# Squared deviation from the row mean, 1024 x 4096 in fp32: two tiles of four rows per partition instead of three loads and four stores

## The chip, the core and the metric

The kernel runs on one core of one Trainium2 chip. A core has several engines with instruction queues of their own: VectorE (DVE in the profile) and ScalarE (ACT) compute here, SyncE (SP) issues the transfers, and 16 DMA engines move data between the chip's memory (HBM) and the core's on-chip memory of 128 partitions. TensorE (PE) and GpSimd (POOL) have no part in the work. The metric is device time in microseconds (us) for one launch, the median of the runs.

## The reference

```python
batch, dim = 1024, 4096
x = np.random.randn(batch, dim).astype(np.float32)

def reference(x, axis):            # axis = -1
    mean = np.mean(x, axis=axis, keepdims=True)
    return ((x - mean) ** 2).astype(np.float32)
```

Each row of 4096 numbers has its mean taken off, and the differences are squared. Input and output are 16.78 MB each.

## The kernel before

Each of the 128 partitions holds 8 consecutive rows of `x`, 16 KiB a row, so that a partition's part of `x` is one run of 128 KiB in HBM. Three loads, all issued at the start by SP (line 44), bring two, four and two rows per partition, in runs of 32, 64 and 32 KiB; each goes into a tile of its own, so nothing is loaded twice and no buffer is used again.

Then a loop goes over the 8 rows of a partition in order. For each row:

- VectorE sums the row, with the sign changed (`reduce_sum`, line 52), and multiplies the sum by 1/4096 (`tensor_scalar_mul`, line 55). This gives `neg_mean`, one number per partition.
- ScalarE squares the row in place, with `neg_mean` as its bias (`activation` with Square, line 56).
- After every second row, SP issues a store of the two finished rows (line 64), in runs of 32 KiB per partition. It waits for ScalarE.

So a row passes VectorE, then ScalarE, then SP's queue; VectorE may be rows ahead of ScalarE. The framework puts in the waits and may move instructions on an engine; it keeps the order in which rows are summed. All seven transfers are on SP's one queue, so stores are queued behind all loads.

Of the kernel before, what the change touches and what calls it, by code (L numbers as in the profile page):

```python
# [2 lines left out]

os.environ.setdefault("NEURON_RT_ULTRASERVER_MODE", "4")

# [4 lines left out]

F32 = mybir.dt.float32


@with_exitstack
def kernel(
    ctx: ExitStack,
    tc: tile.TileContext,
    x: bass.AP,
    axis: bass.AP,
    out: bass.AP,  # L20
):


    nc = tc.nc

    B, D = x.shape
    P = nc.NUM_PARTITIONS
    R = B // P
    LOADS = [2, 4, 2]
    S = 2  # L30
    assert B == P * R and sum(LOADS) == R
    inv_d = 1.0 / float(D)

    x_v = x.rearrange("(p r) d -> p (r d)", p=P)
    out_v = out.rearrange("(p r) d -> p (r d)", p=P)

    io = ctx.enter_context(tc.tile_pool(name="io", bufs=1))
    stats = ctx.enter_context(tc.tile_pool(name="stats", bufs=2 * R))

    rows = []  # L40
    r0 = 0
    for i, n in enumerate(LOADS):
        x_tile = io.tile([P, n * D], F32, tag=f"x{i}")
        nc.sync.dma_start(out=x_tile, in_=x_v[:, r0 * D:(r0 + n) * D])  # L44
        rows += [(x_tile, k) for k in range(n)]
        r0 += n

    for r, (x_tile, k) in enumerate(rows):
        row = x_tile[:, k * D:(k + 1) * D]
        neg_sum = stats.tile([P, 1], F32)  # L50
        neg_mean = stats.tile([P, 1], F32)
        nc.vector.reduce_sum(  # L52
            out=neg_sum, in_=row, axis=mybir.AxisListType.X, negate=True
        )
        nc.vector.tensor_scalar_mul(out=neg_mean, in0=neg_sum, scalar1=inv_d)  # L55
        nc.scalar.activation(  # L56
            out=row,
            in_=row,
            func=mybir.ActivationFunctionType.Square,
            bias=neg_mean,  # L60
            scale=1.0,
        )
        if r % S == S - 1:
            nc.sync.dma_start(
                out=out_v[:, (r + 1 - S) * D:(r + 1) * D],
                in_=x_tile[:, (k + 1 - S) * D:(k + 1) * D],
            )


# [1 line left out]
_INS = ['x', 'axis']  # L71
_OUTS = [((1024, 4096), 'float32')]

_NUMBERS = {'axis': -1}


# [26 lines left out]
```

## Time and profile before

| | us |
|---|---|
| median of 3 runs | 84.35 (84.27 to 84.47) |
| the profiled execution, its own time | 84.35 |
| its span, first to last instruction | 82.6 |
| one sum of a row on VectorE, line 52 | 4.41 |
| one scaling of the sum on VectorE, line 55 | 0.146 |
| one square of a row on ScalarE, line 56 | 3.70 |
| the table load of ScalarE | 1.28 |

The span is what the profile's stretches are measured in: time 0 is the first instruction. What the execution's time has beyond it, 1.78 us, lies around the span. "Landing" is when a transfer's last data has been confirmed. A line of a group of instructions reads: line, engine, operation, output <- input, shapes, count, then busy time in all and the mean of one in ns, then how long the engine had sat idle before them and for what. In order of time, the core of the work on the second load looks like this:

```profile
32.14 8.75 DVE L52 TENSOR_REDUCE neg_sum<-x_tile 128x1 f32<-128x4096 f32 x2 [10.41 <-DMA x_tile<-in_x_dram]
40.81 0.14 DVE L55 TENSOR_SCALAR neg_mean<-neg_sum 128x1 f32<-128x1 f32 x1
40.87 4.41 DVE L52 TENSOR_REDUCE neg_sum<-x_tile 128x1 f32<-128x4096 f32 x1
40.98 3.71 ACT L56 ACTIVATE x_tile<-x_tile,neg_mean 128x4096 f32<-128x4096 f32 x1 [12.04 <-DVE neg_mean L55]
```

The first number of a line is its start, the second how long it lasted, both in us. VectorE waited 10.41 us for the second load to land, and ScalarE 12.04 us for the first mean of it.

### The profile page before, as it was taken

To read this page: it belongs to the slowest core of one execution; us is meant where nothing else is said; L and a number is where in the kernel's file an instruction comes from. 1 tells how busy PE (TensorE), PEld (TensorE's weight loads), DVE (VectorE), ACT (ScalarE), POOL (GpSimd) and SP (SyncE) were. 2 spreads that over 40 slices of the span, in tenths; PEclk is the share of its full clock that TensorE was granted. 3 is DMA by queue.
4 is the path that set the end of the run, shared out by engine and by line. 5 is a ranking of instruction groups with operands and counts; after the bars stand their busy time and mean duration, and the time that the engine had idled before them with its cause. 6 is when DMAs were issued, how large, how long until landed. Compare 5 with 4: busy or idle time off the path is not lost.

```text
span 82.6 us, 83 instructions
## 1 busy us (share of the span) xinstructions
DVE 35.4 (43%) x16; ACT 30.7 (37%) x9; POOL 0.2 (0%) x4
## 2 busy tenths in 40 slices
DVE  0000008999500004999999999999300000000000
ACT  0000006000599900000196978979699800000000
POOL 0000000000000000000000000000000000000000
DMA  8698990999999099799879998997998999799790
GB/s 238 270 413 349 508 730 32 508 508 508 508 508 476 32 508 508 317 444 508 254 302 460 492 413 365 508 444 333 492 492 381 397 508 429 333 508 476 333 460 0
DMA packets 1008, 33.55 MB, mean 406 GB/s; under 512 B 112, under 2 KB 112, under 8 KB 112
## 3 DMA queue, kind: packets, MB, share of 16 engines
q1 hardware_dynamic: 1008, 33.55, 96.1%
HBM read 16.78 MB, written 16.78 MB: 406 GB/s over the span
## 4 chain that ended last, share of the span: by engine, by line
DMA 37%; DVE 32%; ACT 4%; ACTq 4%; SPq 0%; issue 0%
DMA x_tile<-in_x_dram 37%; DVE neg_sum L52 32%; ACT x_tile L56 4%; ACTq L98 4%; SPq L44 0%; DVE neg_mean L55 0%
## 5 line engine op out<-in xcount | busy, mean ns | idle before, releaser
L52 DVE TENSOR_REDUCE neg_sum<-x_tile 128x1 f32<-128x4096 f32 x8 | 35.0, 4411 | 23.2 <-DMA x_tile<-in_x_dram 23.2
L56 ACT ACTIVATE x_tile<-x_tile,neg_mean 128x4096 f32<-128x4096 f32 x8 | 29.4, 3704 | 22.3 <-DVE neg_mean L55 22.3
L56 ACT ACT_TABLE_LOAD x1 | 1.3, 1283 | 12.8 <-DMA x_tile<-in_x_dram 12.8
L55 DVE TENSOR_SCALAR neg_mean<-neg_sum 128x1 f32<-128x1 f32 x8 | 1.1, 146 | 0.0
L84 POOL MEMSET const-bfloat16-1.0<- 128x1 bf16 x1 | 0.1, 101 | 0.0
L84 POOL MEMSET const-uint8-127<- 128x1 uint8 x1 | 0.1, 101 | 0.0
L84 POOL MEMSET const-float32-0.0<- 128x1 f32 x1 | 0.1, 98 | 0.2 <-issue 0.2
L84 POOL MEMSET const-float32-1.0<- 128x1 f32 x1 | 0.1, 98 | 0.0
## 6 DMA issues: line engine op xcount, KB each, us to landing
out_dram<-x_tile SPq DMA_DIRECT2D x4, 4096.0 KB, 15.1
x_tile<-in_x_dram SPq DMA_DIRECT2D x2, 4096.0 KB, 26.7
x_tile<-in_x_dram SPq DMA_DIRECT2D x1, 31.0
```

The costliest lines, as they stand in the source:

```text
L52: nc.vector.reduce_sum(out=neg_sum, in_=row, axis=mybir.AxisListType.X, negate=True)
L55: nc.vector.tensor_scalar_mul(out=neg_mean, in0=neg_sum, scalar1=inv_d)
L56: nc.scalar.activation(out=row, in_=row, func=mybir.ActivationFunctionType.Square, bias=neg_mean, scale=1.0,)
L84: nc = _bacc.Bacc("TRN2", target_bir_lowering=False, num_devices=1)
L98: with _tile.TileContext(nc) as tc:
```

## The change

The 1024 rows are now cut into two halves of 512. In each half a partition holds 4 consecutive rows, 64 KiB, so that a tile is one block of 8.39 MB in HBM. There are two loads and two stores, each of a whole tile, in runs of 64 KiB.

The work on a tile is shared out differently, and its order on VectorE and ScalarE is fixed by hand (`keep_in_program_order`):

- ScalarE takes the mean of row 3 by itself: an `activation` with Identity copies the row into a scratch tile that nothing reads and puts the row's sum into `total`; a second small one multiplies it by -1/4096.
- VectorE takes the means of rows 0, 1 and 2, as before.
- ScalarE squares rows 3, 0, 1 and the first half of row 2.
- VectorE does the second half of row 2, 2048 elements, in two steps: it adds the negative mean, and multiplies the result by itself.
- SP stores the tile when both engines are through with it.

```diff
-    R = B // P
-    LOADS = [2, 4, 2]
-    S = 2
+    Q = 4
+    H = D // 2
+    ntiles = B // (P * Q)
...
-    x_v = x.rearrange("(p r) d -> p (r d)", p=P)
-    out_v = out.rearrange("(p r) d -> p (r d)", p=P)
+    x_t = x.rearrange("(n p q) d -> n p (q d)", p=P, q=Q)
+    out_t = out.rearrange("(n p q) d -> n p (q d)", p=P, q=Q)
...
+    for i in range(ntiles):
+        x_tile = io.tile([P, Q * D], F32)
+        nc.sync.dma_start(out=x_tile, in_=x_t[i])
+        tiles.append(x_tile)
+
+    inorder = tc.keep_in_program_order
+
+    def mean_on_act(row):
+        copy = scratch.tile([P, D], F32)
+        total = stats.tile([P, 1], F32)
+        neg_mean = stats.tile([P, 1], F32)
+        nc.scalar.activation(
+            out=copy, in_=row, func=ACT.Identity, scale=1.0, accum_out=total
+        )
+        nc.scalar.mul(out=neg_mean, in_=total, mul=-inv_d)
+        return neg_mean
+
+    def mean_on_dve(row):
         neg_sum = stats.tile([P, 1], F32)
         neg_mean = stats.tile([P, 1], F32)
-        nc.vector.reduce_sum(
+        inorder(nc.vector.reduce_sum(
             out=neg_sum, in_=row, axis=mybir.AxisListType.X, negate=True
-        )
-        nc.vector.tensor_scalar_mul(out=neg_mean, in0=neg_sum, scalar1=inv_d)
...
+        ))
+        inorder(nc.vector.tensor_scalar_mul(out=neg_mean, in0=neg_sum, scalar1=inv_d))
+        return neg_mean
+
+    def square_on_act(part, neg_mean):
+        inorder(nc.scalar.activation(
+            out=part, in_=part, func=ACT.Square, bias=neg_mean, scale=1.0
+        ))
+
+    for i in range(ntiles):
+        row = [tiles[i][:, q * D:(q + 1) * D] for q in range(Q)]
+        m3 = mean_on_act(row[3])
+        m0 = mean_on_dve(row[0])
+        square_on_act(row[3], m3)
+        m1 = mean_on_dve(row[1])
+        square_on_act(row[0], m0)
+        m2 = mean_on_dve(row[2])
+        square_on_act(row[1], m1)
+        square_on_act(row[2][:, :H], m2)
+        back = row[2][:, H:]
+        nc.vector.tensor_scalar_add(out=back, in0=back, scalar1=m2)
+        nc.vector.tensor_mul(out=back, in0=back, in1=back)
+        nc.sync.dma_start(out=out_t[i], in_=tiles[i])
```

In what follows, tile A is the first tile (`tiles[0]`, load A, store A) and tile B the second.

More of the change, by code (lines that the diff above doesn't have):

```diff
@@ L11 @@
 F32 = mybir.dt.float32
+ACT = mybir.ActivationFunctionType
 @with_exitstack
@@ L27 @@
     P = nc.NUM_PARTITIONS
-    R = B // P
-    LOADS = [2, 4, 2]
-    S = 2
-    assert B == P * R and sum(LOADS) == R
+    Q = 4
+    H = D // 2
+    assert B % (P * Q) == 0
+    ntiles = B // (P * Q)
     inv_d = 1.0 / float(D)
-    x_v = x.rearrange("(p r) d -> p (r d)", p=P)
-    out_v = out.rearrange("(p r) d -> p (r d)", p=P)
[L37 to L46, printed above, removed]
@@ L48 @@
-    for r, (x_tile, k) in enumerate(rows):
-        row = x_tile[:, k * D:(k + 1) * D]
+    x_t = x.rearrange("(n p q) d -> n p (q d)", p=P, q=Q)
+    out_t = out.rearrange("(n p q) d -> n p (q d)", p=P, q=Q)
+    io = ctx.enter_context(tc.tile_pool(name="io", bufs=ntiles))
+    scratch = ctx.enter_context(tc.tile_pool(name="scratch", bufs=1))
+    stats = ctx.enter_context(tc.tile_pool(name="stats", bufs=2 * ntiles * Q))
+    tiles = []
+    for i in range(ntiles):
+        x_tile = io.tile([P, Q * D], F32)
+        nc.sync.dma_start(out=x_tile, in_=x_t[i])
+        tiles.append(x_tile)
@@ L53 @@
             out=neg_sum, in_=row, axis=mybir.AxisListType.X, negate=True
-        )
[L55 to L67, printed above, removed]
+        ))
```

## The prediction

> **What bounds the kernel now.** I read the DMA rows first, since the kernel reads 16.78 MB and writes 16.78 MB and does little with them.
>
> ```profile
> span 82.6 us, 83 instructions
> DVE 35.4 (43%) x16; ACT 30.7 (37%) x9; POOL 0.2 (0%) x4
> DMA  8698990999999099799879998997998999799790
> q1 hardware_dynamic: 1008, 33.55, 96.1%
> ```
>
> Both compute engines idle for more than half of the span; the one DMA queue keeps its 16 DMA engines occupied for 96.1% of it. (The lower digits in the row of tenths are no gaps: in the packet records, below, each DMA engine goes from packet to packet.) Next, the stretches between the landings, cut where one transfer's packets give way to the next's:
>
> ```profile
> 12.24:31.57 19.33, 8.93 (x4) 8.59 (x3) 0.00 (x0) 1.00 0.96 417
> 31.57:42.35 10.78, 10.21 (x4) 1.37 (x1) 0.00 (x0) 1.00 1.02 398
> 42.35:52.03 9.68, 9.68 (x5) 8.32 (x3) 0.00 (x0) 1.00 1.00 433
> 52.03:61.71 9.68, 6.59 (x5) 8.32 (x3) 0.00 (x0) 1.00 1.00 433
> 61.71:71.39 9.68, 0.00 (x0) 4.13 (x2) 0.00 (x0) 1.00 1.00 433
> ```
>
> The columns are the stretch, its length, the busy time of VectorE, ScalarE and GpSimd, the clock, the DMA share and GB/s. These are load 2 (8.39 MB), load 3 (4.19 MB), and stores 1 to 3 (4.19 MB each). A store takes 9.68 us whatever the engines do; load 2, twice the bytes, takes 19.33. One transfer is out of line: load 3 takes 10.78, that is 1.10 more than a store of the same size. In the trace's packet records (each DMA engine moves 8 packets of a transfer, one for each of its 8 partitions) a 32 KiB packet follows the last after 1.21 us and a 64 KiB one after 2.414, and on all 16 DMA engines only the last two packets of load 3 are long, 1.72 and 1.76 us in the mean instead of 1.21, from 38.7 us until they end at 42.0 to 42.7. What is queued behind them is the first store. I call this place the seam: loads end and stores begin. On the DMA engine that ends last it costs 10.946 - 9.68 = 1.27 us. From the first packet at 1.75 us to the last at 81.41 there is no other idle time in those records; the first packets have 0.65 us extra (1.86 against 1.21).
>
> ```profile
> 0.73 1.33 SPq L44 DMA_DIRECT2D x_tile<-in_x_dram  x3
> SPq L64 <- ACT x_tile L56: 49.1, 4, 16.9
> SPq L64 <- DMA x_tile<-in_x_dram: 13.5, 2, 10.7
> DMA to landing us min/median/max: 23.8/23.8/23.8
> ```
>
> Loads are issued at 0.73 and the first packet moves at 1.75: 1.02 us from issue to data. SP's queue does wait for ScalarE, but the last row (the first store, issued at 28.97) shows that its data is taken by 23.8 us later, behind both loads: these waits are hidden. The chain of waits on the page ends through VectorE and ScalarE (32% and 4%), because it follows the last store back to its issue; that store was issued at 65.9 and its packets began only at 71.4, so that chain is not what sets the end. The bytes and the seam are.
>
> **The change, part by part.**
>
> *Packets.* Before: 48 packets of 32 KiB and 8 of 64 KiB for each DMA engine, 48 x 1.2096 + 8 x 2.4137 = 77.37 us. After: 32 of 64 KiB, 77.24. Gain 0.13, if a 64 KiB store packet goes as a 64 KiB load packet does; no row here shows one.
> The Trainium skill (DMA: Bandwidth & Descriptors, Anatomy of one DMA — SWDGE path) fits 2.0 us fixed for each DMA, on another path than SP's; by it three transfers fewer would save 6 us, an estimate. The rows show no such cost between queued transfers: 4 x 9.68 us for the stores is bytes alone.
>
> *The larger first load.* Load A lands at 12.77 (0.73 + 12.0) + 8 x (2.414 - 1.210) = 22.4 us, load B's packets end at 41.04 to 41.40 and it lands at 41.75, provided that the seam takes nothing from it. Nothing is lost by the later start, since the queue has load B to do.
>
> *Work on tile A*, which now decides when the first store can start. Rows:
>
> ```profile
> L52 DVE TENSOR_REDUCE neg_sum<-x_tile 128x1 f32<-128x4096 f32 x8 | 35.0, 4411 | 23.2 <-DMA x_tile<-in_x_dram 23.2
> L56 ACT ACTIVATE x_tile<-x_tile,neg_mean 128x4096 f32<-128x4096 f32 x8 | 29.4, 3704 | 22.3 <-DVE neg_mean L55 22.3
> L56 ACT ACT_TABLE_LOAD x1 | 1.3, 1283 | 12.8 <-DMA x_tile<-in_x_dram 12.8
> L55 DVE TENSOR_SCALAR neg_mean<-neg_sum 128x1 f32<-128x1 f32 x8 | 1.1, 146 | 0.0
> ```
>
> VectorE: three sums with their scaling, one every 4.39 us (45.26 to 49.64), from 22.44 to 35.6. Then an add and a multiply over 128x2048, of which there is no row. VectorE's 4411 ns for 4096 and 146 for 1 element make 1.04 ns an element, so 2.28 us each; at least 1.1 each if it took two elements at a time, at most 4.41 each (a whole row's sum). I take 2.28, the nearest row's rate: VectorE ends at 40.2 (37.8 to 44.4).
> The Trainium skill (VectorE: DVE Perf Modes, The perf-mode tier table) has 1227 ns for an fp32 add of a scalar and 2293 for an fp32 multiply of two tensors at 2048 elements; by it VectorE would end at about 39.2, an estimate.
>
> ScalarE: a row summed, priced as the square (3.71); writing out the sum and scaling it, two small steps without a row, 0.3 (two of VectorE's 146 ns) to 2.6 (two table loads), taken as 0.5; three squares every 3.62; half a square, 1.85 to 3.71, taken as 2.0. From 22.45: 26.7, 37.5, 39.5 (39.1 to 43.3). The means that VectorE delivers at 27.0, 31.4 and 35.6 come before ScalarE needs them (30.3, 33.9, 37.5). The table load sits ahead of any wait for data in the built program, so it lies under the first load's 22 us; if it came behind it, ScalarE would end at 40.8.
>
> The store on SP waits for both engines; behind it SP has only store B, which waits longer anyway. Ready: 40.2 + 1.02 = 41.2, just as load B's packets run out (41.04 to 41.40).
>
> *The seam.* The old cost, 1.27, arose with the store queued 9 us before the loads' last packets; why they slow I can only infer (the store's reading starts beside the load's). Now the store arrives at the very end, so that it can hardly slow two packets of 2.4 us. In its place the store's first packets find an empty pipe. The only row for that is the first load's, 0.65. Bounds: 0, and 1.27 as before. I take 0.65.
>
> *Tile B.* Lands at 41.75, same work: 41.78 + 17.8 = 59.5, store ready at 60.6. Store A's packets end at 41.04 to 41.40 + 0.65 + 19.32 = 61.0 to 61.4: covered by 0.4 to 0.8 us. If store A starts later, so does this limit move, and only one gap is paid.
>
> *Sum.* The last packet ends at 41.38 + 0.65 + 2 x 19.32 = 80.67 instead of 81.41: -0.13 - 1.27 + 0.65 = -0.75. The profiled execution took 84.35 with a span of 82.6, the same as the median of 3. 84.35 - 0.75 = **83.6 us**; in general 82.95 + s, with s the cost of the seam.
>
> **The rivals.**
> *The seam costs as much as before* (s = 1.27): 84.2, no measurable difference (0.2%, 0.17 us, is about what a measurement here can tell). For it: the slow packets may come with any turn from loads to stores, whenever the store was queued. Against: in the records they begin over 3 us before the turn.
> *The first store comes late.* Place: the end of the work on tile A. Price: each us after 41.4 idles all DMA engines, plus 0.65. It decides from s = 1.57, that is ready at 42.3, work that ends at 41.3 instead of 40.2. Halfway to the upper bounds (half a square at 2.9, small steps at 1.5, the add and multiply at 2.9 each) work ends at 41.4 on both engines, s is 41.4 + 1.02 - 41.4 + 0.65 = 1.67, and the time 84.6; at the upper bounds work ends at 44.4, s is 4.67, and the time 87.6. I put the case at 85.0, nearer to the halfway point. For it: three prices have no row. Against: both engines would need their upper half.
> *The slow part grows with the packet.* If the last two packets are slowed by the same share (1.74 / 1.21) they cost 2 x 2.414 x 0.44 = 2.1 to 2.5: 85.2. Against: the store would have to be queued 5 us before the end, and it comes 0.2.
> *The change does nothing to the path* (seam gone, store early enough): s near 0, 82.95. It is the good end of my own case.
>
> **How the numbers follow.** Forecast (s from 0 to 1.0; 82.9 to 84.0) 0.62, seam as before 0.16, late store 0.13, slow part grown 0.09. The first is faster, the second faster by a hair or the same (0.04 and 0.12), the last two slower but for 0.01: faster 0.66, same 0.13, slower 0.21. The range 82.9 to 85.1 leaves out about half of the last two cases and a little below.
>
> **What would show it.** Right: load A lands at 22.4, load B at 41.8 with no long packets at its end; the store of A is issued at 39.5 to 40.3; a hole or a long first packet of about 0.65 us in the DMA records at 41 to 42; none at 61; the end some 0.7 us earlier. The add at 128x2048 and the half square tell the prices I lacked. Wrong: load B landing at 43 (the seam stays), the first store issued after 41.3 (late), store packets of 64 KiB above 2.42 us (the bytes cost more), or a hole at 61.

## The result and the profile after

The changed kernel takes 83.49 us (83.34 to 83.73, 4 runs) against 84.41 us (84.27 to 84.47, 4 runs): a ratio of 0.9896 with a 95% interval of 0.9868 to 0.9924. Run again later, in five rounds beside other kernels, it took 83.68 us against 84.49, a ratio of 0.9904 (0.9886 to 0.9922). It is faster by 0.8 to 0.9 us, about 1%. The profiled execution took 83.34 us, the least of the four, and its span fell from 82.6 to 81.6.

From the page of the changed kernel, the rows that answer to those of before: span, engines, the DMA row in tenths, the queue.

```profile
span 81.6 us, 81 instructions
DVE 34.2 (42%) x16; ACT 34.7 (43%) x15; POOL 0.2 (0%) x4
DMA  9399947999984999993899991999994799999290
q1 hardware_dynamic: 576, 33.55, 95.9%
```

The same bytes go over the same queue, whose share has hardly moved. (In the row of tenths a long packet makes the low digits move about; a hole, that is a stretch in which a DMA engine moves nothing, is read from the packet records, the start and length of every packet in the trace, and from the windows below.) Now the stretches, cut where one whole-tile transfer gives way to the next; the columns are as before.

```profile
21.60:40.90 19.30, 17.11 (x8) 16.71 (x7) 0.00 (x0) 1.00 1.00 435
40.90:60.50 19.60, 17.11 (x8) 16.71 (x7) 0.00 (x0) 1.00 0.99 428
60.50:79.90 19.40, 0.00 (x0) 0.00 (x0) 0.00 (x0) 1.00 1.00 432
```

These are load B, store A and store B. Load B, the last load, now runs at full rate to its end: 19.30 us, twice what a 4.19 MB transfer takes. What is left of the seam lies at the start of the second stretch, which is 0.2 to 0.3 us longer than its neighbours. In the packet records the last packet of load B has its 2.42 us on every DMA engine; then each engine stands idle until the first store packet, 0.19 us in the mean. Before, the last two packets were long, by 1.06 us together in the mean.

The work on tile A, in order of time (start, duration, engine, line):

```profile
22.54 3.62 ACT L55 ACTIVATE copy<-x_tile 128x4096 f32<-128x4096 f32 x1 [20.53 <-DMA x_tile<-in_x_dram]
22.54 4.42 DVE L64 TENSOR_REDUCE neg_sum<-x_tile 128x1 f32<-128x4096 f32 x1 [22.54 <-DMA x_tile<-in_x_dram]
26.06 0.19 ACT L55 ACTIVATION_READ_ACCUMULATOR copy<-x_tile 128x1 f32 x1
26.28 0.20 ACT L58 ACTIVATE neg_mean<-total 128x1 f32<-128x1 f32 x1
26.52 12.80 ACT L71 ACTIVATE x_tile<-x_tile,neg_mean 128x4096 f32<-128x4096 f32 x4
...
36.21 1.29 DVE L86 TENSOR_SCALAR x_tile<-x_tile,neg_mean 128x2048 f32<-128x2048 f32 x1
37.53 2.29 DVE L87 TENSOR_TENSOR x_tile<-x_tile 128x2048 f32<-128x2048 f32 x1
39.90 19.68 SPq L88 DMA_DIRECT2D out_dram<-x_tile  x2
```

ScalarE ends at 39.32, VectorE at 39.82, and SP issues the store at 39.90 (two issues stand in that line: the second starts at 59.24, and the 19.68 runs to its end). The records have its first packet at 41.21; load B's packets ended at 40.96 to 41.52, depending on the DMA engine. So the first store packet comes 1.31 us after the issue, just as the load packets run out. It is not simply the issue that is late: the first DMA engine fell idle at 40.96, 1.06 us after it.

What SP's queue waited for, with times and the longest, in us:

```profile
SPq L88 <- DVE x_tile L87: 57.2, 2, 38.2
SPq L119 <- DMA out_dram<-x_tile: 21.1, 2, 19.3
```

Before, SP waited for ScalarE's squares and that was hidden; now the first store waits for VectorE's multiply, and that wait ends about 1 us before the load packets do. This is the one wait in the kernel that a shorter piece of work could still move to some use.

### The profile page after: what moved, and what is told of

Its sections match the earlier page's. It is cut to its first block, busy times and chain, and to the rows that moved or that the text cites. A ratio compares the mean times of both kernels' runs of the same rounds, so it can differ in the third digit from the quotient of the medians.

```text
span 81.6 us, 81 instructions
## 1 busy us (share of the span) xinstructions
DVE 34.2 (42%) x16; ACT 34.7 (43%) x15; POOL 0.2 (0%) x4
## 4 chain that ended last, share of the span: by engine, by line
DMA 50%; DVE 21%; SPq 0%; issue 0%
DMA x_tile<-in_x_dram 50%; DVE neg_sum L64 16%; DVE x_tile L87 3%; DVE x_tile L86 2%; DVE neg_mean L67 1%; SPq L46 0%
## 5 line engine op out<-in xcount | busy, mean ns | idle before, releaser
L64 DVE TENSOR_REDUCE neg_sum<-x_tile 128x1 f32<-128x4096 f32 x6 | 26.5, 4412 | 24.6 <-DMA x_tile<-in_x_dram 24.6
L71 ACT ACTIVATE x_tile<-x_tile,neg_mean 128x4096 f32<-128x4096 f32 (+1 forms) x8 | 25.6, 3270 | 0.1
L55 ACT ACTIVATE copy<-x_tile 128x4096 f32<-128x4096 f32 x2 | 7.2, 3616 | 23.1 <-DMA x_tile<-in_x_dram 23.1
L87 DVE TENSOR_TENSOR x_tile<-x_tile 128x2048 f32<-128x2048 f32 x2 | 4.6, 2293 | 0.1
L86 DVE TENSOR_SCALAR x_tile<-x_tile,neg_mean 128x2048 f32<-128x2048 f32 x2 | 2.6, 1286 | 0.1
```

The lines of the kernel that those rows point to most:

```text
L55: nc.scalar.activation(out=copy, in_=row, func=ACT.Identity, scale=1.0, accum_out=total)
L64: inorder(nc.vector.reduce_sum(out=neg_sum, in_=row, axis=mybir.AxisListType.X, negate=True))
L71: inorder(nc.scalar.activation(out=part, in_=part, func=ACT.Square, bias=neg_mean, scale=1.0))
L86: nc.vector.tensor_scalar_add(out=back, in0=back, scalar1=m2)
L87: nc.vector.tensor_mul(out=back, in0=back, in1=back)
```

## The experiments

Three theories of the seam were on trial. E: it costs time because a store stands in the queue while load packets are still moving. T: any turn from loads to stores without a hole costs the same. L: the slow packets belonged to the layout or the 32 KiB packets of the kernel before.

**A store queued very early.** In the changed kernel:

```diff
         row = [tiles[i][:, q * D:(q + 1) * D] for q in range(Q)]
+        if i == 0:
+            square_on_act(row[0], mean_on_dve(row[0]))
+            nc.sync.dma_start(out=out_t[i], in_=tiles[i])
+            continue
```

> The changed kernel, but on tile A only row 0 is worked on (rows 1 to 3 of tile A are left out and go to the output as they came), so that the store of A is queued at about 32 us, 9 us before load B's packets run out. Theory E (the seam costs time because the store stands in the queue while load packets still move): the slow last load packets come back, load B lands at 43.0 or later, and the time is 83.07 + 1.27 = about 84.3; if the slow part grows with the packet, 85.3. Theory T (any turn from loads to stores without a hole costs the same, however long the store was queued): 84.3 too. Theory L (the slow packets belonged to the layout or the 32 KiB packets of the kernel before): load B lands at 41.9 and the time is about 83.1.

Measured: 84.41 us, a ratio of 1.0005 to the kernel before (0.9987 to 1.0023); 0.9 us slower than the changed kernel though it does less work (rows 1 to 3 of tile A go out as they came). From its timeline, and its time from issue to landing of load B:

```profile
31.20 0.35 SPq L79 DMA_DIRECT2D out_dram<-x_tile  x1
```

```profile
DMA to landing us min/median/max: 22.1/32.0/42.0
```

The same row of the changed kernel:

```profile
DMA to landing us min/median/max: 21.8/31.2/40.7
```

The last number is load B's: with the store queued early it lands 1.3 us later. In the packet records the last 64 KiB packet of each DMA engine takes 3.08 to 3.68 us instead of 2.42, 0.98 us too long in the mean. So L falls: layout and packets are those of the changed kernel. And the cost did not double with the packet: it is 0.98 us in one packet of 64 KiB, where it was 1.06 us in two of 32 KiB. Nor did it grow with the time that the store stood in the queue: the load packet before the last has its 2.42 us on every engine, though the store was issued some 10 us before the loads ended. Theory T expected the same time, so this run doesn't tell E from T.

**The kernel before, with a later first store.** Its loop written out, with the order on VectorE and ScalarE fixed by hand; row 1 is scaled only after row 2 is summed:

```diff
-    for r, (x_tile, k) in enumerate(rows):
...
+    scale(0, reduce(0))
+    square(0)
+    late = reduce(1)
+    s2 = reduce(2)
+    scale(1, late)
+    square(1)
+    scale(2, s2)
+    square(2)
+    for r in range(3, R):
+        scale(r, reduce(r))
+        square(r)
```

> The kernel before with one scaling on VectorE moved behind the next row's sum, so that row 1 is squared at 36.6 to 40.3 and the first store comes into the queue at 41.3 to 41.6 instead of 30, just when load 3's packets run out. Theories E and T: load 3 takes 9.7 us instead of 10.78, no long packets, a hole of 0.2 to 0.6 in its place, time 84.4 - 1.27 + 0.2 to 0.6 = 83.3 to 83.7. Theory L: load 3 still takes 10.8 us and the time is 84.4 or more.

Measured: 83.53 us, a ratio of 0.9895 (0.9878 to 0.9911). Loads, layout, packets and sharing of the work are those of the kernel before; what is new is the order, above all the place of one small instruction. Its first store's issue and the stretch from the end of load 2 to the middle of the seam:

```profile
40.41 0.35 SPq L71 DMA_DIRECT2D out_dram<-x_tile  x1
```

```profile
31.30:40.90 9.60, 8.75 (x4) 4.23 (x2) 0.00 (x0) 1.00 1.01 437
```

The DMA share is 1.01. The same stretch in the kernel before has 1.12, which is the mark of long packets: two begin in it and their whole time is counted there.

```profile
31.30:40.90 9.60, 8.76 (x4) 0.00 (x0) 0.00 (x0) 1.00 1.12 437
```

Load 3's packets end at 40.98 to 41.45 instead of 42.01 to 42.69, none of them long, and a hole of 0.2 us in the mean follows. So the whole gain of the change, 0.9 us, is had by delaying one store by 11 us. This refutes L a second time.

**Loads of four and four alone.** In the kernel before:

```diff
-    LOADS = [2, 4, 2]
+    LOADS = [4, 4]
```

> The kernel before with loads of four and four rows, all else as before (four stores of 32 KiB runs, partition pitch 128 KiB). The first store is issued at about 38.7 and queued at 40.0, 1.1 us before load B's packets run out. Theory E: at most a part of the old cost, 0 to 0.5, time 83.1 to 83.6, and store packets follow load packets with no hole. Theory T: a turn without a hole costs 1.27: 84.3. Theory L, if the pitch is what matters: 84.3; if the 32 KiB load packets: 83.1.

Measured: 83.24 us, a ratio of 0.9858 (0.9844 to 0.9873), faster than the changed kernel. The first store is issued at 39.57, not at 38.7 as expected, so it leads the end of the load packets by less than was planned. No load packet at the seam is long; the store packets follow with 0.04 us of idle time in the mean. A turn with next to no hole and no cost: T falls. And a store in the queue while load packets still move (they end at 40.84 to 41.56) need not cost anything, so E holds only for a store that comes earlier than this one. The timeline around the issue shows why the store comes when it does: it needs rows 0 and 1 alone, and row 1's mean is scaled (35.66) only after row 2's sum, so that its square starts at 35.84.

```profile
35.66 0.15 DVE L55 TENSOR_SCALAR neg_mean<-neg_sum 128x1 f32<-128x1 f32 x1
35.72 4.41 DVE L52 TENSOR_REDUCE neg_sum<-x_tile 128x1 f32<-128x4096 f32 x1
35.84 3.71 ACT L56 ACTIVATE x_tile<-x_tile,neg_mean 128x4096 f32<-128x4096 f32 x1 [0.68 <-DVE neg_mean L55]
39.57 27.65 SPq L64 DMA_DIRECT2D out_dram<-x_tile  x4
```

The store follows that square at once. That this falls on a good moment comes from the order that the framework chose.

**A store one packet early.** The changed kernel with row 2 of tile A left as it came (the last four lines of work are done `if i > 0`).

> The changed kernel, but row 2 of tile A is not squared (it goes to the output as it came), so that ScalarE ends tile A at 37.4 and the store of A is queued at 38.7, 2.4 us (one packet of 64 KiB) before load B's packets run out. Theory E: between the costs at 1 us and at 9 us of lead, 0.3 to 1.0: time 83.4 to 84.1. Theory T: 84.3. Theory L: 83.1.

Measured: 84.15 us, a ratio of 0.9969 (0.9952 to 0.9986). The time is just above the 83.4 to 84.1 that E had given. The store's issue:

```profile
37.63 0.35 SPq L89 DMA_DIRECT2D out_dram<-x_tile  x1
```

The last load packets are 0.90 us too long in the mean: nearly the whole cost, though the store was issued 6.4 us later than in the first experiment. These are records of the slowest of ten executions, 84.54 us. A second loss is in it: load B lands as late as 43.27, so tile B is late by as much, and store B is issued at 60.65, after which some DMA engines stand idle shortly (0.08 us in the mean over all holes; at the seam itself there is none).

**Between the two.** The same (add and multiply on tile A still left out), but with 1024 elements of row 2 squared. Against the changed kernel, the line that differs from the last run:

```diff
-        square_on_act(row[2][:, :H], m2)
+        square_on_act(row[2][:, :H if i > 0 else 1024], m2)
```

> The changed kernel, but of row 2 of tile A only 1024 elements are squared (the other 3072 go out as they came), so that the store of A is issued at 38.5 and queued at 39.8: between the run with four stores behind loads of four and four (issued 39.57, no long packets) and the one without row 2 (issued 37.63, last packets 0.9 us long). Theory E with reading that starts as soon as the store is queued: the last load packet is slowed for its last 1.2 to 1.7 us alone, 0.3 to 0.6 us of excess, time 83.4 to 83.7. If there is a threshold instead (a packet is slowed wholly or not at all): 83.1 or 84.0.

Measured: 83.98 us, a ratio of 0.9946 (0.9929 to 0.9964). The store's issue:

```profile
38.55 0.35 SPq L89 DMA_DIRECT2D out_dram<-x_tile  x1
```

The last load packets are 0.38 us too long in the mean, inside the 0.3 to 0.6 that was expected, and on single DMA engines anything from 0.06 to 0.66: a packet can be slowed in part. The time alone would not show it. It is 0.3 above what I expected and fits the 84.0 of a threshold; the profiled execution, with these packets, was the fastest of the four, 83.77 us. The means hide that the DMA engines are not in step: the one that ends load B last does so at 42.02, 0.5 later than in the changed kernel, and the end waits for the last.

**A later store, work shared less evenly.** The changed kernel with the whole of row 2 on ScalarE:

```diff
-        square_on_act(row[2][:, :H], m2)
-        back = row[2][:, H:]
-        nc.vector.tensor_scalar_add(out=back, in0=back, scalar1=m2)
-        nc.vector.tensor_mul(out=back, in0=back, in1=back)
+        square_on_act(row[2], m2)
```

> The changed kernel with all of row 2 squared on ScalarE (the add and multiply on VectorE undone). ScalarE ends tile A at 37.4 + 3.7 = 41.0, the store of A is queued at 42.3, 0.8 to 1.3 us after load B's packets run out (41.0 to 41.5). If a late store idles the DMA engines for just as long as it is late: a hole of 1.1 us in the mean, time 83.07 + 1.1 = 84.2 (84.0 to 84.4), that is 0.7 above the changed kernel; if a first packet costs 0.65 more, as the prediction priced it, 84.8. If the sharing of the work does not matter because transfers hide it: 83.5.

Measured: 83.90 us, a ratio of 0.9934 (0.9912 to 0.9956). The store's issue:

```profile
41.35 0.35 SPq L85 DMA_DIRECT2D out_dram<-x_tile  x1
```

Its first packets move at 42.2, 0.85 after issue, on DMA engines that had all fallen idle by 41.8; a hole of 0.93 us in the mean. Its profiled execution took 84.07 us, inside what was expected, the median 0.1 below. There is no extra 0.65: the first store packets take 2.46 us against 2.42.

**The stores alone, work as before.** Loads of four and four, and `S = 4`: a store waits for four rows.

> Two loads and two stores of 64 KiB runs with the old division of the work (VectorE sums all rows, ScalarE squares all). Tile A ends at 47.6 (four sums behind load A at 22.6, four squares), the store of A is queued at 48.9, 7.6 us after load B's packets: time 83.07 + 7.6 = 90.7 (90.2 to 91.5). That would show that the sharing of work is needed only because the store waits for four rows. If the old division is enough: 83.5.

Measured: 90.43 us (one run). The store is issued at 47.72:

```profile
40.38 7.31 ACT L56 ACTIVATE x_tile<-x_tile,neg_mean 128x4096 f32<-128x4096 f32 x2 [0.68 <-DVE neg_mean L55]
...
47.72 0.35 SPq L64 DMA_DIRECT2D out_dram<-x_tile  x1
```

The 7.35 us of idle DMA engines in its records are the whole of the loss, as near as can be told (90.43 - 7.35 = 83.08). So the new sharing of the work is what makes two large stores bearable. That it gains anything beside that no run shows: loads of four and four with four stores go without it and are faster.

**Packet size alone.** The changed kernel with each store cut into two of 32 KiB runs, issued together:

```diff
-        nc.sync.dma_start(out=out_t[i], in_=tiles[i])
+        for c in (1, 0):
+            half = slice(c * 2 * D, (c + 1) * 2 * D)
+            nc.sync.dma_start(out=out_t[i][:, half], in_=tiles[i][:, half])
```

> The changed kernel with each store cut into two with runs of 32 KiB, both issued when the whole tile is ready (39.9), so that only size and number of the packets change. By the packet records (1.2096 against 2.414/2 us) 0.07 to 0.1 us: time 83.5 to 83.6, the same as the changed kernel within what can be measured. If each transfer had a fixed cost of its own of 1 to 2 us: 85.5 to 87.5. Long last load packets: none, as in the changed kernel.

Measured: 83.62 us, a ratio of 0.9902 (0.9887 to 0.9916): between the two times of the changed kernel. Two stores more cost nothing that can be measured.

**Three kernels side by side**, five rounds each:

> The changed kernel again, beside the next two on the same chip: 83.4 to 83.6, first store issued at 39.9, holes of 0.1 to 0.7 us at 41.0 to 41.6.

> Loads of four and four, with the work and the four stores of the kernel before: 83.2 to 83.3, 0.2 below the changed kernel, because its first store is issued 0.3 us earlier and neither leaves a hole nor slows a load packet. If the difference seen before was chance: the same time as the changed kernel.

> The changed kernel with the split of row 2 at 2304 instead of 2048 (ScalarE takes 2304, VectorE 1792). VectorE ends tile A at 39.4 and ScalarE at 39.55, so the store of A is issued at 39.6 instead of 39.9, as in the run with loads of four and four. If the time of issue against the end of load B is all that separates those two: 83.2 to 83.3, holes shorter by 0.3 us. If the four smaller stores matter: 83.5.

| kernel | first store issued | idle at the seam, mean | us | ratio to before (95%) |
|---|---|---|---|---|
| changed | 40.09 | 0.22 | 83.68 | 0.9904 (0.9886 to 0.9922) |
| loads of four and four | 39.64 | 0.02 | 83.24 | 0.9847 (0.9830 to 0.9863) |
| changed, split at 2304 | 39.75 | 0.04 | 83.32 | 0.9853 (0.9838 to 0.9868) |

The intervals of the last two do not touch that of the first. The timeline of the split at 2304:

```profile
36.41 1.15 DVE L86 TENSOR_SCALAR x_tile<-x_tile,neg_mean 128x1792 f32<-128x1792 f32 x1
37.60 2.02 DVE L87 TENSOR_TENSOR x_tile<-x_tile 128x1792 f32<-128x1792 f32 x1
39.75 0.35 SPq L88 DMA_DIRECT2D out_dram<-x_tile  x1
```

Moving 256 elements from VectorE to ScalarE, so that both end together, takes 0.41 us off the add and the multiply (1.29 + 2.29 against 1.15 + 2.02), gets the store out 0.34 us sooner and is worth about as much. Their times agree although one has four stores and the other two. The version to keep is the plain one: the kernel before with `LOADS = [4, 4]`, a single line, 1.25 us (1.5%) faster than it and faster than the changed kernel.

All points of the seam together, from the packet records of one profiled execution each, beside the median time of all executions of that run (idle is the mean over the DMA engines of their holes; long is how much the last load packets of an engine exceed their usual time, in the mean):

| first store issued | kernel | long | idle | us, median |
|---|---|---|---|---|
| 28.97 | before | 1.06 | 0.02 | 84.4 |
| 31.20 | very early store | 0.98 | 0.01 | 84.41 |
| 37.63 | one packet early | 0.90 | 0.08 | 84.15 |
| 38.55 | between | 0.38 | 0.08 | 83.98 |
| 39.57 | loads of four and four | 0.01 | 0.04 | 83.24 |
| 39.90 | changed | 0.00 | 0.19 | 83.49 |
| 40.41 | before, later store | 0.03 | 0.20 | 83.53 |
| 41.35 | row 2 on ScalarE | 0.00 | 0.93 | 83.90 |
| 47.72 | stores alone | 0.00 | 7.35 | 90.43 |

Where nothing slows the load packets, they end at 40.8 to 41.8, each DMA engine at its own time. The 0.08 in the rows of 37.63 and 38.55 lies between store A and store B. Down the table the time falls as the store comes later, and from 39.9 on it rises; the best place tried is 39.6 to 39.75, 1.3 to 2 us before the last load packets end. Between 38.55 and 39.57 nothing was tried.

## Why the prediction was right

- *What bounds it: bytes and the seam.* Right. With the mean losses of the table (long and idle) taken off, all the times come to 83.0 to 83.5 us.
- *Packets, -0.13.* Not told apart from nothing: stores of 32 and of 64 KiB runs gave the same time.
- *Load A at 22.4, load B at 41.75 with no long packets.* Measured 22.52 and 41.87, and none. Both are 0.12 late from the start: the first packets took 0.70 us extra instead of 0.65 (3.12 against 2.42 us), and the rest is scatter between runs, whose load A lands at 22.5 to 22.8.
- *The work on tile A, to 40.2.* Measured 39.82. The multiply (2.29 against 2.28), the half square (1.99 against 2.0) and ScalarE's small steps (0.39 and their gaps against 0.5) were priced well. Two terms were off and partly cancelled. The add took 1.29 us, not 2.28: the rate of a sum is not that of an add. Beyond the 146 ns of a single element, the add takes 0.56 ns an element where the sum takes 1.04. Here the Trainium skill was the better source (VectorE: DVE Perf Modes, The perf-mode tier table, 1227 ns; this trace 1286). And the three sums came every 4.52 us instead of 4.39 (22.54, 27.06, 31.58), since in the order fixed by hand each scaling follows its own sum and starts when it has ended (26.99, the sum ending at 26.96); before, the framework had let the scaling lag one sum behind, and it started before the sum ahead of it had ended (45.19 against 45.28).
- *Issue to data, 1.02.* That was the first load's. A store that finds idle DMA engines moves 0.84 to 0.85 us after its issue (later store, row 2 on ScalarE, stores alone). But in the changed kernel itself the first store packet moves 1.31 us after the issue, when some engines had been idle since 40.96; why it took longer there stays open. That it moved at 41.21, just when the prediction had the store ready (41.2), is luck: the work ended 0.4 us earlier and the way from there to the first packet took 0.4 longer.
- *The seam, 1.27 replaced by 0.65.* The direction and the reason were right, and this is the term that was mis-sized. I took 0.65 from the first load, as if an empty pipe had to be filled. The first store packets take 2.45 us in the mean, 0.03 longer than others; nearly all that is lost is the hole, 0.19 us in the mean. With 0.2 for it and 0.12 for the later loads, 82.95 becomes 83.3, which is what the profiled execution took (83.34). That the median, 83.49, lies so near to 83.6 is in part luck: the seam was priced 0.46 too high, and the later loads and the scatter between executions (83.34 to 83.73) made up for most of it.
- *Tile B covered by 0.4 to 0.8 us.* Right: store B was issued at 59.24, and in the changed kernel the store packets go on at 60.6 to 61.1 without a hole.
- *The rivals.* "As before" is refuted for a store that arrives this late, and holds for one that arrives early (84.41). "Grown with the packet" is refuted: 0.98 in a 64 KiB packet. "Late store" is real but cheaper than I put it near its beginning, for want of the 0.65: 0.4 us for 1.45 us of later issue, and then about one for one (6.5 us more for the next 6.37). One reason given against it was wrong: both engines would not have needed their upper half, since the store waits for the later of the two, and one late engine is enough.

What stays open is why a waiting store slows the last load packets. The records fit a store that begins to read on-chip memory while the load's last 64 KiB per DMA engine are still coming: the loss is about the same in bytes for both packet sizes (0.98 to 1.06 us, some 27 KB at 64 KiB in 2.414 us), and it shrinks as the store comes later. No record shows the reading itself, so this is an inference.

## What to carry to other kernels

When transfers fill the whole span, an earlier store need not be a better one: look at the turn from loads to stores in the packet records, and let the first store be issued shortly before the last load packets end (here 1.3 to 2 us). Time made free on compute engines is then worth only what it moves that one issue, and the cheapest lever that moves it (here the sizes of the loads) is the one to use. Price an unknown instruction by its kind and not by its element count from another kind.

## What the runs showed of the hardware that was not expected

- A store queued behind loads costs the loads' last 64 KiB per DMA engine 0.9 to 1.06 us in the mean when it is issued at 28.97 to 37.63, with 32 KiB and 64 KiB packets alike, and 0.01 when it is issued at 39.57; a load queued behind a load costs nothing (load B behind load A: 19.30 us for 8.39 MB).
- The first store packets on DMA engines that stood idle for 7 us take hardly longer than others (2.46 against 2.42 us), while the first load packets of the changed kernel carry 0.70 us.
- An `activation` that also sums its input (Identity, 3.62 us for 4096 elements) is no slower than the square with a bias (3.69 to 3.71), and reads the sum out in an instruction of its own, 0.19 us.
